# The order of the gated values of two expert rows on VectorE and ScalarE

## The chip, the cores and the metric

The kernel runs as one program on one core of a Trainium2 chip. The metric is the device time of one execution in microseconds (us). Three executions of the kernel before were timed, and one more was profiled.

## The reference

Two transformer blocks are computed for one sequence of 256 tokens of width 1024, in float32. The change lies in the last layer of the second block, a product-key expert layer: 16384 experts, 8 heads, and 16 experts chosen per head and token.

```python
u = jnp.take(expert_down, ei, axis=0)
act = jax.nn.gelu(jnp.einsum("btd,bthkd->bthk", xi, u), approximate=False)
vv = jnp.take(expert_up, ei, axis=0)
return jnp.einsum("bthk,bthkd->btd", (gi * act), vv)
```

After it come the residual sum and one last rmsnorm. `ei` are the experts that were chosen, `gi` their softmax gates.

## The kernel before, in words

The kernel gathers nothing: it computes every expert for every token and multiplies by a gate that is zero where an expert was not chosen. The experts form 128 *rows* of 128 experts. For a row c, `down_gen` computes gelu(down . x) for all 256 tokens, a tile `ge` of 128 experts x 256 tokens (PE into `dps`, then ScalarE). A dense table of gates G lies in device memory and is fetched 8 rows at a time into `gr` (1 MB, three buffers). `hidden(c)` then makes the gated values of two rows, c and c + 1, called a *pair* here, and `ts_row` multiplies a row with the matching 128 x 1024 block of `up`, into four PSUM banks `acc` that run over all 128 rows.

Every float32 operand is split into a high part (rounded, written by ScalarE) and a low part (the rest, written by VectorE), and a product is three matmuls: high.high, low.high, high.low. The names are:

- `ge`: the gelu of a row, then, in place, the gated value (VectorE, SCALAR_TENSOR_TENSOR `ge<-ge,gr`).
- `ph`, `pl`: high and low part of the gated values of a pair (ScalarE ACTIVATE `ph<-ge`; VectorE TENSOR_TENSOR `pl<-ge,ph`). Two buffers each.
- `wr`: a raw weight load of two rows (1 MB, three buffers), issued on SP's queue; `wh`, `wl`: high and low part of one row of weights (ScalarE `wh<-wr`; VectorE `wl<-wr,wh`). Three buffers each, a buffer for a row.
- `held`: the same for the last four rows of `up`, which have buffers of their own.

A row costs PE 12 matmuls of 512 columns (2 token tiles x 2 halves x 3 products), so a pair costs 24.

The stage has three parts. While rows of `down` are left, each pass of the loop in `experts` does one pair of `up` rows and two rows of `down` (26 passes). Then 36 passes do `up` rows alone. The last two pairs (rows 124 to 127) aren't multiplied in the loop: their weights go to `held`, and `final` (line 1932) multiplies them token tile by token tile (12 matmuls of pair 124, 12 of pair 126 for tile 0, then 24 for tile 1), so that the last norm of tile 0 can run beside the matmuls of tile 1.

The order on every engine is the order in which the program issues the work. In a pass, `hidden(c + 2)` comes ahead of the matmuls of pair c (line 1715), and a planner (`top_up`, line 300) issues the splits of the weights some rows ahead of their use, by a model of when their inputs are there. In an `up`-only pass ScalarE thus gets ph, ph, wh, wh, and VectorE ge, pl, ge, pl, wl, wl. An engine runs its instructions in this order, and one that waits holds up all that stand behind it. Nearly all VectorE and ScalarE work is recorded through one helper, line 123; matmuls are line 163, loads line 173.

Of the kernel before, what the change touches and what calls it, by code (L numbers as in the profile page):

```python
# [9 lines left out]
F32 = mybir.dt.float32  # L10
# [4 lines left out]
AF = mybir.ActivationFunctionType  # L15
ALU = mybir.AluOpType
# [110 lines left out]
class Net:  # L127
# [1545 lines left out]
    def experts(self, tab, down, gd):  # L1673
        ve, a = self.ve, self.a
        acc = self.acc4()

        G = gd.tile([N_EXP_CH // GC, P, S, GC], F32, name="G")
        with self.tc.tile_pool(name="pb", bufs=3) as pb:
            self.weave([self.build_G(G, tab, pb, acc)], self.some(down, RING - KEEP))

        groups = []

        def fetch():
            if len(groups) < N_EXP_CH // GC:
                t = gr.tile([P, S, GC], F32, tag="gr", name="gr")
                self.clock.slot("gr", 3, t)
                self.load(t, G[len(groups)])
                groups.append(t)

        def hidden(c):  # L1690

            ph = pw.tile([P, 2, S], F32R, tag="ph", name="ph")
            pl = pw.tile([P, 2, S], F32R, tag="pl", name="pl")
            for e in range(2):
                g = self.ge.pop(c + e)
                ve.scalar_tensor_tensor(out=g, in0=g, scalar=1.0 / GSC, in1=groups[c // GC][:, :, c % GC + e],
                                        op0=ALU.mult, op1=ALU.mult)
                self.split_to(ph[:, e, :], pl[:, e, :], g)
            return ph, pl

        with self.tc.tile_pool(name="pw", bufs=2) as pw, self.tc.tile_pool(name="ph", bufs=1) as pool:
            views = pool.tile([P, 8, 1024], F32R, name="held")
            hold = [[views[:, 2 * j, :], views[:, 2 * j + 1, :]] for j in range(4)]
            self.hold = lambda: hold.pop(0)
            late = []
            with self.tc.tile_pool(name="gr", bufs=3) as gr:
                for n in range(KEEP - 3, -1, -2):
                    self.drain(self.some(down, RING - n))
                    fetch()
                self.drain(self.some(down, RING))  # L1710
                p = hidden(0)
                for c in range(0, N_EXP_CH, 2):
                    cur, last = p, c >= N_EXP_CH - 4
                    if c + 2 < N_EXP_CH:
                        p = hidden(c + 2)
                    if c % GC == GC - 2:
                        fetch()
                    if last:
                        late.append(([self.take("u") for _ in range(2)], cur))
                    else:  # L1720
                        for e in range(2):
                            self.ts_row(acc, self.take("u"), cur[0], cur[1], e, c == 0 and e == 0, False)
                    for _ in range(2):
                        self.drain(self.some(down, len(self.ge) + 1))
            self.hold = None
            self.final(acc, late)
# [393 lines left out]
```

## Time and profile before

| | us |
|---|---|
| three timed executions | 1568.54, 1565.62, 1569.11 (median 1568.54) |
| the profiled execution | 1565.99 |
| its span, first to last instruction | 1564.2 |
| passes with `up` and `down` | 1037.6 to 1329.7 |
| passes with `up` alone | 1329.7 to 1539.9 |
| the last four rows on PE | 1539.9 to 1556.0 |
| last norm of tile 1 and its store | 1556.0 to 1564.2 |

Times in the trace count from the first instruction of the span. Engines are PE (TensorE matmul), PEld (its weight load), DVE (VectorE), ACT (ScalarE), POOL and SP. Matmuls overlap in the pipeline: one of 512 columns is shown with 0.39 us, and the next starts some 0.23 us after it, so PE's pace is read from the starts. Idle time is shown with what ended it; where an instruction waits for two things, the one named is the one that came last by the trace's reckoning.

### The profile page before, as it was taken

The page shows a single profiled execution, that of the slowest core. Times are in us where ns is not written, and L with a number is a line of the kernel's source. Part 1 is how long each engine was busy: PE and PEld are TensorE (multiplying, and loading weights), DVE is VectorE, ACT ScalarE, POOL GpSimd, SP SyncE. Part 2 cuts the span into 40 slices and gives each one's busy share as a digit, 9 for nine tenths or more (in the row PEclk, how much of TensorE's full clock was granted, in tenths as well). Part 3 has the DMA queues.
Part 4 walks back from the last instruction along what each step waited for, and adds up shares of the span by engine and source line. Part 5 has one row for each costly group of instructions (what it writes and reads, how often), then busy time and mean ns, then how long its engine had stood idle before and what let it go on. Part 6 is the DMA issues. An engine that isn't in the chain of part 4 may idle for free.

```text
span 1564.2 us, 25831 instructions
## 1 busy us (share of the span) xinstructions
PE 1501.6 (96%) x10234; PEld 1351.0 (86%) x10234; DVE 1043.1 (67%) x1949; ACT 779.8 (50%) x1295; POOL 450.8 (29%) x354
## 2 busy tenths in 40 slices
PE   8999899999999999999999999899999999999997
PEld 7878888998698989898999999899999999877775
DVE  6567454646668887556798877755656565777776
ACT  5655444555555342346556555544545454444443
POOL 4433643445666555467780000000000000000000
PEclk9999999999999999999999999999999999999999
DMA  6652555555434333256445687876666555665652
GB/s 229 234 182 59 191 186 188 187 190 193 180 113 139 131 109 109 95 176 255 162 160 191 216 250 240 271 263 216 215 216 216 204 200 216 238 220 215 226 178 94
DMA packets 103785, 295.35 MB, mean 189 GB/s; under 512 B 5744, under 2 KB 39024, under 8 KB 100720
## 3 DMA queue, kind: packets, MB, share of 16 engines
q1 hardware_dynamic: 70640, 276.93, 50.4%
q10 hardware_dynamic: 33024, 16.78, 3.7%
q8 instruction: 80, 1.31, 0.3%
q14 instruction: 41, 0.34, 0.1%
HBM read 275.86 MB, written 17.83 MB: 188 GB/s over the span
## 4 chain that ended last, share of the span: by engine, by line
PE 68%; DVE 16%; ACT 6%; issue 6%; POOL 2%; DMA 1%; SPq 0%; ACTq 0%; POOLq 0%; DVEq 0%
PE dps L163 21%; PE acc L163 18%; PE wsps L163 13%; PE fps L163 4%; DVE wl L123 3%; ACT wh L123 3%; PE yps L163 3%; DVE ge L123 3%; POOL wl L123 1%; ACT ph L123 1%; DVE eq L123 1%; DVE pl L123 1%; DVE rt L123 1%; PE tp L168 1%; PE pu L163 1%
## 5 line engine op out<-in xcount | busy, mean ns | idle before, releaser
L123 DVE TENSOR_TENSOR wl<-wr,wh 128x1024 fp32r<-128x1024 f32 (+1 forms) x298 | 365.3, 1245 | 193.2 <-ACT wh L123 192.8
L123 ACT ACTIVATE wh<-wr 128x1024 fp32r<-128x1024 f32 (+1 forms) x436 | 445.0, 1040 | 53.1 <-ACT wh L123 25.6
L123 POOL TENSOR_TENSOR wl<-wr,wh 128x512 fp32r<-128x512 f32 (+2 forms) x276 | 367.1, 1354 | 312.2 <-ACT wh L123 301.3
L163 PE MATMUL dps<-xh,wh 128*128 128x256 f32 x1024 | 251.5, 283 | 0.0
L163 PE MATMUL dps<-xl,wh 128*128 128x256 f32 x1024 | 251.3, 283 | 0.0
L123 POOL TENSOR_TENSOR xn<-h,gain 128x512 f32<-128x512 f32 x4 | 5.1, 1274 | 742.9 <-DVE h L123 737.3
L163 PEld LDWEIGHTS dps<-xl,wh 128*128 128x128 f32 x1024 | 196.7, 192 | 1.0
L163 PEld LDWEIGHTS dps<-xh,wh 128*128 128x128 f32 x1024 | 196.6, 192 | 1.0
L163 PE MATMUL acc<-wh,ph 128*128 128x512 f32 x496 | 196.1, 395 | 0.9 <-ACT ph L123 0.8
L163 PE MATMUL acc<-wh,pl 128*128 128x512 f32 x496 | 194.0, 391 | 0.0
L163 PE MATMUL wsps<-xh,wh 128*128 128x256 f32 x680 | 178.9, 298 | 0.0
L163 PE MATMUL wsps<-xl,wh 128*128 128x256 f32 x680 | 171.9, 288 | 0.0
L163 PE MATMUL acc<-wl,ph 128*128 128x512 f32 x496 | 156.6, 397 | 2.0
L163 PE MATMUL dps<-xh,wl 128*128 128x256 f32 x1024 | 145.3, 284 | 2.3 <-DVE wl L123 1.4
L123 ACT ACTIVATE ge<-dps 128x256 f32<-128x256 f32 x128 | 49.2, 384 | 187.0 <-PE dps L163 186.9
L163 PEld LDWEIGHTS wsps<-xh,wh 128*128 128x128 f32 x680 | 133.7, 197 | 1.2 <-issue 0.4
L163 PEld LDWEIGHTS dps<-xh,wl 128*128 128x128 f32 x1024 | 131.9, 192 | 2.9 <-DVE wl L123 1.6
L163 PEld LDWEIGHTS wsps<-xl,wh 128*128 128x128 f32 x680 | 133.9, 197 | 0.1
L123 ACT ACTIVATE ph<-ge 128x256 fp32r<-128x256 f32 x128 | 53.5, 418 | 145.1 <-DVE ge L123 111.1
L163 PEld LDWEIGHTS acc<-wl,ph 128*128 128x128 f32 x496 | 90.7, 188 | 32.7 <-DVE wl L123 15.3
L163 PEld LDWEIGHTS acc<-wh,ph 128*128 128x128 f32 x496 | 93.2, 188 | 25.9 <-ACT wh L123 7.1
L163 PEld LDWEIGHTS acc<-wh,pl 128*128 128x128 f32 x496 | 93.3, 188 | 18.2 <-DVE pl L123 0.3
(437 smaller groups left out, 2606.6 us busy)
## 6 DMA issues: line engine op xcount, KB each, us to landing
wr<-in_down_dram SPq DMA_DIRECT2D x64, 1024.0 KB, 5.0
wr<-in_up_dram SPq DMA_DIRECT2D x64, 1024.0 KB, 5.0
wr<-in_w_in_a_dram SPq DMA_DIRECT2D x35, 1024.0 KB, 4.9
wr<-in_w_mlp_out_dram SPq DMA_DIRECT2D x16, 1024.0 KB, 4.9
G<-st ACTq DMA_DIRECT2D x16, 1024.0 KB, 6.0
gr<-G SPq DMA_DIRECT2D x16, 1024.0 KB, 6.9
wr<-in_w_mlp_in_dram SPq DMA_DIRECT2D x14, 1024.0 KB, 5.0
wr<-in_w_z_dram SPq DMA_DIRECT2D x8, 1024.0 KB, 4.9
```

The costliest lines, as they stand in the source:

```text
L123: return f(*args, **kw)
L163: self.nc.tensor.matmul(out=out, lhsT=lhsT, rhs=rhs, start=start, stop=stop)
L168: self.nc.tensor.transpose(out, in_, self.ident[:in_.shape[0], :in_.shape[0]])
```

## The change

In `hidden`, the two gated values are made first (each followed, on the other engine, by its high part), and then both low parts. The operations, their operands and their count stay the same. 

```diff
-            for e in range(2):
-                g = self.ge.pop(c + e)
+            gs = [self.ge.pop(c + e) for e in range(2)]
+            for e, g in enumerate(gs):
                 ve.scalar_tensor_tensor(out=g, in0=g, scalar=1.0 / GSC, in1=groups[c // GC][:, :, c % GC + e],
                                         op0=ALU.mult, op1=ALU.mult)
-                self.split_to(ph[:, e, :], pl[:, e, :], g)
+                self.ac.activation(out=ph[:, e, :], in_=g, func=AF.Copy)
+            for e, g in enumerate(gs):
+                ve.tensor_tensor(out=pl[:, e, :], in0=g, in1=ph[:, e, :].bitcast(F32), op=ALU.subtract)
             return ph, pl
```

VectorE in one `up`-only pass, pair 120 (`ge_14336` and `ge_14367` are its two rows, `wl_16100` and `wl_16116` the low parts of its weights). Before:

```order
L123 SCALAR_TENSOR_TENSOR ge_14336<-ge_14336,gr_15759 128x256
L123 TENSOR_TENSOR pl_16090<-ge_14336,ph_16089 128x256
L123 SCALAR_TENSOR_TENSOR ge_14367<-ge_14367,gr_15759 128x256
L123 TENSOR_TENSOR pl_16090<-ge_14367,ph_16089 128x256
L123 TENSOR_TENSOR wl_16100<-wr_16013,wh_16099 128x1024
L123 TENSOR_TENSOR wl_16116<-wr_16013,wh_16115 128x1024
```

VectorE at the same place, now:

```order
L123 SCALAR_TENSOR_TENSOR ge_14336<-ge_14336,gr_15759 128x256
L123 SCALAR_TENSOR_TENSOR ge_14367<-ge_14367,gr_15759 128x256
L123 TENSOR_TENSOR pl_16090<-ge_14336,ph_16089 128x256
L123 TENSOR_TENSOR pl_16090<-ge_14367,ph_16089 128x256
L123 TENSOR_TENSOR wl_16100<-wr_16013,wh_16099 128x1024
L123 TENSOR_TENSOR wl_16116<-wr_16013,wh_16115 128x1024
```

The second gated value moves ahead of the first low part; it is so in all 64 pairs. ScalarE's order there (ph, ph, wh, wh) and PE's, POOL's and SP's in the whole program are as before.

The one other difference lies at the end of the loop, on VectorE and ScalarE alike. VectorE before (`ge_14550`, `ge_14581` are pair 124, `ge_14656`, `ge_14687` pair 126; `wr_16097` holds the weights of pair 124, `wr_16139` those of pair 126):

```order
L123 TENSOR_TENSOR held_11647<-wr_16097,held_11647 128x1024 x2
L123 SCALAR_TENSOR_TENSOR ge_14550<-ge_14550,gr_15759 128x256
L123 TENSOR_TENSOR pl_16178<-ge_14550,ph_16177 128x256
L123 SCALAR_TENSOR_TENSOR ge_14581<-ge_14581,gr_15759 128x256
L123 TENSOR_TENSOR pl_16178<-ge_14581,ph_16177 128x256
L123 TENSOR_TENSOR held_11647<-wr_16139,held_11647 128x1024 x2
L123 SCALAR_TENSOR_TENSOR ge_14656<-ge_14656,gr_15759 128x256
L123 TENSOR_TENSOR pl_16214<-ge_14656,ph_16213 128x256
L123 SCALAR_TENSOR_TENSOR ge_14687<-ge_14687,gr_15759 128x256
L123 TENSOR_TENSOR pl_16214<-ge_14687,ph_16213 128x256
```

VectorE there now:

```order
L123 TENSOR_TENSOR held_11647<-wr_16097,held_11647 128x1024 x2
L123 TENSOR_TENSOR held_11647<-wr_16139,held_11647 128x1024
L123 SCALAR_TENSOR_TENSOR ge_14550<-ge_14550,gr_15759 128x256
L123 SCALAR_TENSOR_TENSOR ge_14581<-ge_14581,gr_15759 128x256
L123 TENSOR_TENSOR pl_16180<-ge_14550,ph_16179 128x256
L123 TENSOR_TENSOR pl_16180<-ge_14581,ph_16179 128x256
L123 TENSOR_TENSOR held_11647<-wr_16139,held_11647 128x1024
L123 SCALAR_TENSOR_TENSOR ge_14656<-ge_14656,gr_15759 128x256
L123 SCALAR_TENSOR_TENSOR ge_14687<-ge_14687,gr_15759 128x256
L123 TENSOR_TENSOR pl_16214<-ge_14656,ph_16213 128x256
L123 TENSOR_TENSOR pl_16214<-ge_14687,ph_16213 128x256
```

The planner's reckoning of time moved too, and it puts the split of row 126 ahead of the gated values of pair 124. ScalarE has the same: before held x2, ph x2 (pair 124), held x2, ph x2 (pair 126); now held x3, ph x2, held, ph x2.

## Rows read from the trace of the kernel before

**Rows 1.** Page, part 1: busy us, share of the span, instructions.

```profile
PE 1501.6 (96%) x10234; PEld 1351.0 (86%) x10234; DVE 1043.1 (67%) x1949; ACT 779.8 (50%) x1295; POOL 450.8 (29%) x354
```

**Rows 2.** Windows: stretch, us, busy us of each engine, PEclk, DMA share, GB/s.

```profile
1100.00:1200.00 100.00, 100.00 (x644) 91.50 (x643) 60.36 (x72) 48.25 (x72) 0.00 (x0) 1.00 0.60 211
1329.67:1343.30 13.63, 13.63 (x63) 11.27 (x62) 10.04 (x15) 6.21 (x10) 0.00 (x0) 1.00 0.69 240
1343.30:1539.92 196.62, 194.50 (x806) 146.19 (x804) 145.05 (x200) 92.13 (x134) 0.00 (x0) 1.00 0.58 208
1539.92:1546.37 6.45, 3.94 (x15) 2.39 (x14) 4.88 (x8) 2.73 (x4) 0.00 (x0) 1.00 0.00 0
1546.37:1549.79 3.42, 3.42 (x9) 2.67 (x8) 0.62 (x2) 0.42 (x1) 0.00 (x0) 0.50 0.58 153
1549.79:1555.95 6.16, 6.15 (x27) 4.70 (x25) 4.36 (x14) 2.35 (x6) 1.47 (x2) 1.00 0.00 0
```

**Rows 3.** Waits of PEld, 1343 to 1540: us in total, times, longest.

```profile
PEld acc L163 <- DVE wl L123: 15.3, 31, 0.5
PEld acc L163 <- ACT wh L123: 7.1, 30, 0.5
```

**Rows 4.** Waits of DVE, 1332 to 1540.

```profile
DVE pl L123 <- ACT ph L123: 36.3, 70, 0.8
DVE wl L123 <- ACT wh L123: 18.4, 35, 0.5
```

**Rows 5.** Timeline of DVE, one pass: start us, us, what; in brackets idle before.

```profile
1406.42 0.66 DVE L123 SCALAR_TENSOR_TENSOR ge<-ge,gr 128x256 f32<-128x256 f32 x1
1407.62 0.43 DVE L123 TENSOR_TENSOR pl<-ge,ph 128x256 fp32r<-128x256 f32 x1 [0.55 <-ACT ph L123]
1407.96 0.64 DVE L123 SCALAR_TENSOR_TENSOR ge<-ge,gr 128x256 f32<-128x256 f32 x1
1409.08 0.42 DVE L123 TENSOR_TENSOR pl<-ge,ph 128x256 fp32r<-128x256 f32 x1 [0.48 <-ACT ph L123]
1410.04 2.36 DVE L123 TENSOR_TENSOR wl<-wr,wh 128x1024 fp32r<-128x1024 f32 x2 [0.53 <-ACT wh L123]
1412.31 0.67 DVE L123 SCALAR_TENSOR_TENSOR ge<-ge,gr 128x256 f32<-128x256 f32 x1
```

**Rows 6.** Timeline of ACT, the same pass.

```profile
1407.17 0.42 ACT L123 ACTIVATE ph<-ge 128x256 fp32r<-128x256 f32 x1 [2.11 <-PE acc L163]
1408.63 0.42 ACT L123 ACTIVATE ph<-ge 128x256 fp32r<-128x256 f32 x1 [1.05 <-DVE ge L123]
1408.96 1.99 ACT L123 ACTIVATE wh<-wr 128x1024 fp32r<-128x1024 f32 x2
```

**Rows 7.** Chain that ended last, 1332 to 1564: first and last of 33.

```profile
1345.95 1.22 DVE wl L123
...
1535.11 1.22 DVE wl L123
```

**Rows 8.** Timeline of PE: a row's first matmul (three rows), first matmul of `final`.

```profile
1329.67 0.40 PE L163 MATMUL acc<-wh,ph 128*128 128x512 f32 x1
...
1332.41 0.39 PE L163 MATMUL acc<-wh,ph 128*128 128x512 f32 x1
...
1343.30 0.39 PE L163 MATMUL acc<-wh,ph 128*128 128x512 f32 x1
...
1539.92 0.39 PE L163 MATMUL acc<-held,ph 128*128 128x512 f32 x1
```

**Rows 9.** Tiles `wh` and `gr`, 1330 to 1540: duration min/median/max in ns.

```profile
L123 DVE TENSOR_TENSOR wl<-wr,wh x70: 1216/1222/1228, 1333.1 to 1535.1; 128x1024 fp32r<-128x1024 f32 x70
L123 DVE SCALAR_TENSOR_TENSOR ge<-ge,gr x71: 630/651/681, 1329.5 to 1538.5; 128x256 f32<-128x256 f32 x71
```

**Rows 10.** Waits of SP's queue, 1330 to 1564, and DMA issues there.

```profile
SPq L173 <- DVE wl L123: 170.8, 34, 5.5
wr<-in_up_dram SPq DMA_DIRECT2D x34, 1024.0 KB, 5.0
```

**Rows 11.** Last four rows: the wait of PE, the split of pair 124 on DVE.

```profile
PE acc L163 <- ACT ph L123: 2.5, 1, 2.5
1536.25 2.35 DVE L123 TENSOR_TENSOR held<-wr,held 128x1024 fp32r<-128x1024 f32 x2
```

## The prediction

> **What bounds the kernel now.** I read the busy shares first: PE is busy 96% of the span [rows 1], so a change on DVE and ACT pays only where PE waits, or is paced, by them. The windows by stage come next. While `up` and `down` rows alternate PE is busy 100.00 of 100 us [rows 2]: there the 26 pairs can gain nothing. In the passes with `up` alone PE still reads 194.50 of 196.62 us busy [rows 2], which looks full, but a matmul's duration covers part of the gap behind it. So I go by starts: the first five rows of this stage, 60 matmuls, start between 1329.67 and 1343.30 [rows 8], which is 0.2272 us a matmul, 2.73 a row, 5.45 a pair. From there on the chain of waits shows the low part of a pair's second weight row 33 times, from 1345.95 to 1535.11 [rows 7]: 189.16 / 32 = 5.91 us a pair. PE waits 31 times for `wl` and 30 for `wh` [rows 3], at every pair. The stage is paced by something 0.46 us slower than PE.
>
> That is the ring between DVE and ACT. In one pass [rows 5, 6]: DVE makes the first gated value (1406.42), ACT its high part (1407.17), DVE waits 0.55 and makes the low part (1407.62), then the second value (1407.96), ACT its high part (1408.63), and only behind that in ACT's order come the high parts of the weights (1408.96), on which DVE's 2.36 us of `wl` wait (1410.04), and behind these the next pair's first value (1412.31). Once round is 5.89 us. DVE is busy for 145 of the 197 us [rows 2], but all its idle time stands in this ring: 36.3 us for `ph` in 70 waits, 18.4 for `wh` in 35 [rows 4].
>
> **The change part by part.** No instruction is added or removed. In the ring the second gated value moves ahead of the first low part.
>
> Step 1, the new ring, with the durations and distances of that pass. First value 1406.42 to 1407.08, its high part 1407.17 to 1407.59, as before. The second value starts 0.09 us before the end of the instruction ahead of it, as it did behind `pl`: 1406.99 to 1407.63. Its high part follows 0.03 later (1408.63 behind 1408.60 before): 1407.66 to 1408.08. The first low part has its input at 1407.62 as before and ends at 1408.05; the second starts 0.03 behind the second high part, 1408.11, and ends at 1408.53. `wh` starts 0.33 after that high part's start, 1407.99; `wl` 1.08 after that, 1409.07, by when DVE is free. It ends at 1411.43, and the next first value starts at 1411.34. Once round is 4.92 us instead of 5.89: what goes is 0.97, the first low part and most of the wait for `ph`.
>
> Step 2, what is late next. 4.92 is under PE's 5.45, so PE sets the pace and 0.53 us a pair remains as slack. The stage's 36 pairs then take 36 x 5.452 = 196.3 us from 1329.67 and end at 1525.95 instead of 1539.92 [rows 8]: 13.97 us.
>
> Can the buffers hold PE's pace? The row three back frees `wh` and `wl`, two row times (5.45 us) before a row starts; `wh` and then `wl` need some 1.05 + 1.2 of that. `ph` comes free when the pair two back ends, one pair time ahead. And the loads: SP waits 34 times for `wl` to free a `wr` buffer, 170.8 us in all [rows 10], so it is ahead; a load lands in 5.0 us, and with three buffers of a pair there is more than a pair time. At PE's pace in the first 13.63 us the DMA moved 240 GB/s at a share of 0.69 [rows 2], so the rate asked for has been there. Cost: nothing.
>
> Step 3, an overlap that the trace before doesn't show: the second value runs on DVE beside the first high part on ACT. The nearest rows are `wl`, of which one runs beside `wh` and one mostly alone: 1216 to 1228 ns over 70 of them [rows 9], no stretch. The gated values themselves lie between 630 and 681 [rows 9]. So from 0 to 0.05 us a pair, and I take 0; even ten times the upper end would just use up the slack of 0.53. A gain is excluded since a pair runs at PE's pace either way.
>
> Step 4, the last four rows. PE's 48 matmuls start at 1539.92 and the last one ends at 1555.95 [rows 2, 8]; at 0.2272 each they take 48 x 0.2272 + 0.16 (a last one lasts 0.39) = 11.07 instead of 16.03: 4.96 us are lost there. 2.5 of them are one wait for `ph` of pair 126 [rows 11]. Behind this idle the granted clock is 0.50, the lower level of 1.2 GHz, for 3.42 us [rows 2], which is 1.71 us of work. The rest, 0.75, are short waits at pair 124. All three come from DVE arriving late out of the ring. Once it has slack, take T as the time when PE ends pair 122. The weight buffer for row 123 comes free at T - 8.2 (three rows), its `wl` ends about T - 5.9. Then DVE has three `held` splits at 1.18 [rows 11], to T - 2.4; two values, to T - 1.1; two low parts, the second of them when ACT has given the high part, to T - 0.2. The last `held` waits for ACT, which has it at T + 0.4 behind the high parts of pair 124, and ends at T + 1.6; the next value ends at T + 2.2 and its high part at T + 2.6. PE asks for that after 12 matmuls, T + 2.73. It asks for the low part at T + 2.95 and gets it about T + 3.1: a wait of 0.15 at most, too short beside the 2.5 to expect the lower clock. The moved `held` split costs 1.2 us of DVE ahead of pair 124's values; the slack covers it, and without cover it would make PE start pair 124 later by about as much. Gain 4.8, bounds 0 and 4.96.
>
> Step 5, the first pair, where PE waits for `hidden(0)`: the first high part is where it was, the first low part 0.02 later at most (step 1). Nothing.
>
> Behind PE's last matmul the norm of tile 1 stays as it is. The sum: 13.97 + 4.8 = 18.8 us off the profiled execution's 1565.99 (span 1564.2 and 1.8 around it), 1547.2. That execution lies 2.6 under the median of the three timed ones, 1568.54, and the four together have their middle at 1567.3; I set the sum against that: 1548.5.
>
> **The rivals.** A is the forecast. B: the middle gains, the end doesn't. If DVE doesn't get ahead in time, PE still idles before pair 126 and the clock still falls: 1567.3 - 14.0 = 1553.3, or between the two. For it: the end's slack is a sum of small distances, and the order there changed as well. Against it: 0.53 us a pair over 36 pairs.
>
> C: nothing comes of it, because buffers and not the order make the ring. ACT's rows say so on their face: the first `ph` shows 2.11 us idle ended by "PE acc" [rows 6], as if PE had still to free a buffer. Then ACT would start no earlier and the time stays at 1567.3. Against it: `ph` starts 0.09 us behind the end of the gated value, 1407.08, whichever releaser is named, and PE is itself waiting for `wh` and `wl` [rows 3]. The Trainium skill, Perfetto Trace Analysis, section Optimization Strategy, says that the same gap repeated on the engine that should be full can mean that there are too few buffers for the next tile. By that rule the order would be worth nothing and the sum would be 1567.3; by the row it is 18.8 us. The gap does repeat here, but its releasers are splits and not PE, so this trace doesn't bear the rule out.
>
> D, slower: DVE and ACT, now reading the same tile side by side, hold each other up. The place is the second value beside the first high part and the second high part beside the first low part. Decisive is 0.97 us a pair, what the ring gains. If the second value (0.64) and its high part (0.42) took twice as long the ring would be 5.98, 0.07 a pair over 36 pairs: 1567.3 + 2.5, with later starts at the end 1571. The rows of `wl` speak against it (step 3).
>
> **How the numbers follow.** A 0.76, B 0.14, C 0.05, D 0.03; 0.02 for a middle gain of half the size. A measurement of this kernel tells about 0.2% (3.1 us) from no change. A, B and the half gain are faster: 0.92. C is the same: 0.05. D is slower: 0.03. The range goes from A against the lowest execution with 2 us for scatter, 1565.6 - 18.8 - 2 = 1544.8, to B with as much, about 1556.
>
> **What would show it.** In the profile after: DVE's wait `pl<-ph` in the `up`-only passes falls from 36.3 us to a few; one pair takes 5.45 us there, and PE's waits for `wl` and `wh` go; ACT's and DVE's idle is now ended by PE, since they wait for buffers; the last rows start near 1526; PE has no idle of 2.5 us there and the clock stays at 1.00. Step 1 is wrong if a pair still takes 5.9 with the same instructions in the new order; step 2 if a pair takes between 5.5 and 5.9 and PE waits for a load or a buffer; step 4 if PE still idles before pair 126 while the middle has sped up. A time above 1560 would make the reading of the ring wrong.

## The result and the profile after

Four executions of each kernel are compared: before 1568.54, 1565.62, 1569.11 and 1561.81 us (median 1567.08), after 1547.85, 1544.70, 1548.35 and 1546.56 us (median 1547.20). The ratio is 0.9872, with a 95% interval of 0.9857 to 0.9887: some 20 us faster, between 17.7 and 22.4. The forecast was 1548.5.

The profiled execution after has a span of 1546.1 us, 18.1 less than the one before. Its busy shares hardly tell the two apart; this line answers to [rows 1]:

```profile
PE 1487.0 (96%) x10234; PEld 1355.1 (88%) x10234; DVE 1043.8 (68%) x1949; ACT 784.8 (51%) x1295; POOL 450.4 (29%) x354
```

The windows by stage do, with the same columns as [rows 2]: the passes with `up` and `down`, all the passes with `up` alone, the last four rows, and what follows them.

```profile
1100.00:1200.00 100.00, 100.00 (x645) 91.52 (x645) 59.71 (x73) 49.98 (x72) 0.00 (x0) 1.00 0.59 209
1330.90:1526.76 195.86, 195.86 (x866) 162.17 (x865) 158.01 (x218) 102.78 (x147) 0.00 (x0) 1.00 0.63 226
1526.76:1537.81 11.05, 11.04 (x49) 8.80 (x47) 7.52 (x19) 3.12 (x8) 1.41 (x2) 1.00 0.18 47
1537.81:1546.07 8.26, 0.00 (x0) 0.00 (x0) 3.16 (x12) 1.94 (x5) 1.15 (x1) 0.70 0.34 128
```

The `up`-only passes take 195.86 us instead of 210.25 (1329.67 to 1539.92 before): 14.4 less. The last four rows take 11.05 instead of 16.0: 5.0 less, at a granted clock of 1.00 throughout. The first stage doesn't change, and neither does the end behind PE's last matmul (8.26 and 8.3). Against these 19.4 us stands that the `up` passes begin 1.23 us later in this execution, as the whole expert stage does; that lies ahead of the changed code, and the start of this stage lies between 1033.5 and 1038.9 in the profiled executions below.

VectorE over one pass, against [rows 5]:

```profile
1406.40 1.20 DVE L123 SCALAR_TENSOR_TENSOR ge<-ge,gr 128x256 f32<-128x256 f32 x2
1407.74 0.78 DVE L123 TENSOR_TENSOR pl<-ge,ph 128x256 fp32r<-128x256 f32 x2
1409.04 1.23 DVE L123 TENSOR_TENSOR wl<-wr,wh 128x1024 fp32r<-128x1024 f32 x1 [0.52 <-ACT wh L123]
1410.70 1.23 DVE L123 TENSOR_TENSOR wl<-wr,wh 128x1024 fp32r<-128x1024 f32 x1 [0.44 <-ACT wh L123]
1411.85 1.23 DVE L123 SCALAR_TENSOR_TENSOR ge<-ge,gr 128x256 f32<-128x256 f32 x2
```

ScalarE in the same pass, against [rows 6]:

```profile
1407.28 0.77 ACT L123 ACTIVATE ph<-ge 128x256 fp32r<-128x256 f32 x2 [2.05 <-PE acc L163]
1407.96 1.04 ACT L123 ACTIVATE wh<-wr 128x1024 fp32r<-128x1024 f32 x1
1409.61 1.06 ACT L123 ACTIVATE wh<-wr 128x1024 fp32r<-128x1024 f32 x1 [0.61 <-PE acc L163]
```

The two values, the two high parts and the two low parts each run through without a gap. From one pass to the next it is 5.45 us (1406.40 to 1411.85), not 5.89. The waits between 1332 and 1526 answer to [rows 4]; first VectorE's, then ScalarE's:

```profile
DVE wl L123 <- ACT wh L123: 32.9, 69, 0.5
DVE pl L123 <- ACT ph L123: 0.2, 1, 0.2
```

```profile
ACT ph L123 <- PE acc L163: 69.9, 34, 2.2
ACT wh L123 <- PE acc L163: 20.1, 34, 0.6
ACT ph L123 <- DVE ge L123: 2.7, 2, 2.5
```

The wait `pl<-ph` is gone (36.3 to 0.2; with the gaps for which the view names no releaser, VectorE is idle for 4.5 us ahead of `pl`). ScalarE is now held by PE twice a pass: `ph` and the second `wh` wait for a buffer that PE still reads. Before, "PE acc" stood beside `ph` too, but there `ph` came 0.09 us behind the gated value; now it comes 0.23 us behind it (1406.40 and 0.65 for the first value, to 1407.28), and PE is the one waited for. For [rows 3] and the PE line of [rows 11] there is nothing to show: PE and its weight loads wait for nobody from 1325 us to the end. The chain of waits says the same in one line:

```profile
1331.99 205.83 PE acc L163 x908
```

### The profile page after: what moved, and what is told of

It reads as the page before. It is cut to its first block, busy times and chain, and to the rows that moved or that the text cites. A ratio compares the mean times of both kernels' runs of the same rounds, so it can differ in the third digit from the quotient of the medians.

```text
span 1546.1 us, 25831 instructions
## 1 busy us (share of the span) xinstructions
PE 1487.0 (96%) x10234; PEld 1355.1 (88%) x10234; DVE 1043.8 (68%) x1949; ACT 784.8 (51%) x1295; POOL 450.4 (29%) x354
## 3 DMA queue, kind: packets, MB, share of 16 engines
q8 instruction: 80, 1.31, 0.3%
## 4 chain that ended last, share of the span: by engine, by line
PE 80%; DVE 11%; ACT 3%; issue 3%; POOL 2%; DMA 1%; SPq 0%; DVEq 0%; POOLq 0%; ACTq 0%
PE acc L163 30%; PE dps L163 21%; PE wsps L163 13%; PE fps L163 4%; PE yps L163 3%; POOL wl L123 1%; ACT wh L123 1%; DVE eq L123 1%; DVE rt L123 1%; PE tp L168 1%; PE pu L163 1%; POOL hl L123 1%; PE ops L163 1%; PE sc L163 1%; DVE wl L123 1%
## 5 line engine op out<-in xcount | busy, mean ns | idle before, releaser
L123 ACT ACTIVATE wh<-wr 128x1024 fp32r<-128x1024 f32 (+1 forms) x436 | 451.8, 1043 | 92.6 <-PE acc L163 69.6
L163 PE MATMUL acc<-wl,ph 128*128 128x512 f32 x496 | 152.8, 389 | 0.0
L163 PEld LDWEIGHTS acc<-wh,ph 128*128 128x128 f32 x496 | 93.2, 188 | 19.4 <-ACT ph L123 1.0
L163 PE MATMUL wsps<-xh,wl 128*128 128x256 f32 x680 | 98.4, 288 | 0.0
```

Of the source, the lines that this page charges most:

```text
L123: return f(*args, **kw)
L163: self.nc.tensor.matmul(out=out, lhsT=lhsT, rhs=rhs, start=start, stop=stop)
```

## The experiments

The theory: in the `up`-only passes VectorE and ScalarE pass work to each other in a ring of 5.9 us a pair. The new order makes it 4.92, below PE's 5.45, and the slack carries over into the last four rows. The rivals: the new order helps everywhere a little; buffers that PE holds make the ring; the last rows gain by the order that the planner changed there; GpSimd or VectorE contention eats what is gained. Each kernel was timed beside the kernel before and profiled once; the ratios are to the kernel before, with 95% intervals. Where a diff below has a condition, the new order of the change stands under it and the old one under the else. "Up-only passes" is the time from their first matmul to the first one of the last four rows, "last four rows" from there to the end of PE.

**New order from row 52 on (shown), and new order up to there (c < 52).**

```diff
+            if c >= 52:
...
+            else:
...
```

> New order only for pairs from row 52 on, that is in the passes with up alone and the last four rows; the 26 passes before keep the old order. Theory (the DVE-ACT ring paces the up-only passes and nothing else): the whole gain, ratio to the kernel before 0.987, up-only passes 196 us, last four rows on PE 11 us. Rival (the earlier low start of the second value helps everywhere a little): about half the gain, 0.993.

> New order only for the pairs of rows 0 to 51, made in the passes with up and down rows. Theory: no change, ratio 1.000 within 0.2%, up-only passes 210 us, last four rows 16 us. Rival (helps everywhere): 0.993.

From row 52 on: ratio 0.9883 (0.9856 to 0.9911), `up`-only passes 195.87 us, last four rows 11.06: the whole gain. Up to row 52: 0.9995 (0.9981 to 1.0010), 210.24 and 15.96 us. The second shows where the wait goes. VectorE's waits from 1040 to 1325, in the passes with `up` and `down`, first with the old order there (the first of these kernels), then with the new one:

```profile
DVE wl L123 <- ACT wh L123: 86.9, 76, 2.3
DVE pl L123 <- ACT ph L123: 24.2, 50, 0.5
```

```profile
DVE wl L123 <- ACT wh L123: 110.4, 77, 2.4
DVE pl L123 <- ACT ph L123: 1.7, 7, 0.5
```

The same wait goes here as well, 22.5 us of it, and the next wait on the same engine takes 23.5 more. These passes last 292.06 us either way, since PE is full. The rival that it helps everywhere falls.

**Three buffers for the high part, old order.**

```diff
-            ph = pw.tile([P, 2, S], F32R, tag="ph", name="ph")
+            ph = pw.tile([P, 2, S], F32R, tag="ph", name="ph", bufs=3)
```

> Old order, three buffers for the high part of the gated values instead of two. Theory (the order makes the ring; the buffer was free, and 'ended by PE acc' is only the name of the second semaphore): no change, ratio 1.000 within 0.2%, a pair still 5.9 us. Rival C (ACT waits for PE to free the buffer): most of the gain, 0.988 to 0.991, a pair 5.45 us.

Ratio 0.9977 (0.9965 to 0.9988), `up`-only passes 207.85 us, 5.835 a pair, last four rows 15.60. The buffer rival falls: the passes gain 2.4 of 14.4 us. But "no change" was wrong too. Its ScalarE in one pass:

```profile
1412.09 0.42 ACT L123 ACTIVATE ph<-ge 128x256 fp32r<-128x256 f32 x1 [2.06 <-DVE ge L123]
1413.55 0.42 ACT L123 ACTIVATE ph<-ge 128x256 fp32r<-128x256 f32 x1 [1.04 <-DVE ge L123]
1413.88 2.00 ACT L123 ACTIVATE wh<-wr 128x1024 fp32r<-128x1024 f32 x2
```

and its VectorE:

```profile
1411.39 0.67 DVE L123 SCALAR_TENSOR_TENSOR ge<-ge,gr 128x256 f32<-128x256 f32 x1
1412.54 0.43 DVE L123 TENSOR_TENSOR pl<-ge,ph 128x256 fp32r<-128x256 f32 x1 [0.48 <-ACT ph L123]
```

The first `ph` starts 0.03 us behind the end of the value (1411.39 + 0.67 = 1412.06 to 1412.09), where it was 0.09 [rows 5, 6]. With a third buffer the program has no wait for PE at this instruction any more. The wait cost 0.06 us in 34 of the 36 pairs though PE had long been done, and 0.34 in one, for a reason that stays open; together that is the 2.4 us.

**One more operation in the ring (shown), and two (2 in place of the first 1).** The result of the added operation is read by nobody.

```diff
                 self.ac.activation(out=ph[:, e, :], in_=g, func=AF.Copy)
+                for _ in range(1 if e == 0 else 0):
+                    junk = pw.tile([P, S], F32, tag="pj", name="pj")
+                    ve.scalar_tensor_tensor(out=junk, in0=self.x[0][:, 0, :].bitcast(F32), scalar=1.0, in1=groups[c // GC][:, :, c % GC + 1],
+                                            op0=ALU.mult, op1=ALU.mult)
```

> The new order with one more VectorE multiply of 128x256 between the two gated values of each pair, into a scratch tile that nobody reads. Theory (ring 4.92 us, PE 5.45, slack 0.53): the ring gets about 0.57 longer, 5.49, just over PE: 0 to 3 us slower than the changed kernel, ratio to the kernel before 0.987 to 0.989. Rival (the ring is far below PE's pace, or the slack comes from buffers): no DVE wait for ACT's split of the gated values appears and nothing changes at all; rival (no slack): 0.57 x 36 = 20 us, ratio 1.000.

> The same with two more multiplies. Theory: the ring is 4.92 + 1.14 = 6.06 us, above PE's 5.45 and above the old 5.91; up-only passes 213 to 216 us, the last four rows again 16 us, total 2 to 6 us above the kernel before, ratio 1.003. Rival (DVE has much room, it was busy for 74% of these passes only): nothing or 1 us above the changed kernel, 0.988.

The time of a pair is read here on VectorE, from pass to pass. One more: ratio 0.9885 (0.9869 to 0.9902), a pair 5.483 us (forecast 5.49), `up`-only passes 196.40. Two more: 1.0041 (1.0022 to 1.0059), a pair 6.082 (forecast 6.06), passes 216.28 (forecast 213 to 216), last four rows 15.51, and PE waits again, 32 times each for `wl` and `wh`. VectorE with one more:

```profile
1410.21 0.65 DVE L123 SCALAR_TENSOR_TENSOR ge<-ge,gr 128x256 f32<-128x256 f32 x1
1410.77 0.67 DVE L123 SCALAR_TENSOR_TENSOR pj<-xh,gr 128x256 f32<-128x256 f32 x1
1411.34 0.66 DVE L123 SCALAR_TENSOR_TENSOR ge<-ge,gr 128x256 f32<-128x256 f32 x1
```

The added operation moves the second value by 0.57 us (1410.77 to 1411.34). With none the passes run at PE's 5.44 and the ring can't be seen; with one it is 5.48, with two 6.08. Back from these by 0.57 and 1.14 it is 4.91 and 4.94 us, what step 1 had worked out (4.92). So the slack is 0.5 us a pair, and DVE, busy for 158 of 196 us, has no more room than that. With one more operation the last four rows take 13.45 us instead of 11.05, and PE waits there for `ph` and `pl` for 1.8 us in four waits, at a granted clock of 1.00. That part was not in the expectation. Two things stand behind it. VectorE ends the last low part of the passes 4.5 us before PE begins the last rows, where it was 6.0 in the changed kernel and 3.6 in the kernel before: 36 pairs at 0.04 us over PE's pace have used up 1.5 us of its lead. And the added operations stand in the last two pairs too, one of them (0.57 us) ahead of the first high part of pair 126.

**The last two pairs in the old order (shown), and only they in the new (c >= 124).**

```diff
+            if c < 124:
...
+            else:
...
```

> New order everywhere but in the last two pairs, rows 124 to 127. Theory (the end gains because DVE comes out of the up-only passes with slack): up-only passes 196 us; at the end each old pair costs DVE some 0.97 us again, so the high part of pair 126 comes about 0.5 us after PE asks for it; no lower clock; last four rows 11.5 to 12 us, total 0.5 to 1 us above the changed kernel. Rival (the end gains by its own order): the 2.5 us wait and the lower clock are back, last four rows 16 us, total 5 us above it.

> New order only in the last two pairs. Theory: up-only passes stay 210 us; at the end DVE is late by about 2 x 0.97 us less, so PE waits for pair 126 some 0.6 to 1.5 us instead of 2.5; last four rows 12 to 14 us, total 2 to 4 us under the kernel before, ratio 0.998. Rival (the end gains by its own order): last four rows 11 us, ratio 0.9968.

Old order at the end: ratio 0.9896 (0.9875 to 0.9917), passes 195.87, last four rows 12.04 us, and PE's wait there is

```profile
PE acc L163 <- ACT ph L123: 0.4, 1, 0.4
```

close to the forecast of 0.5 us. New order only at the end: 0.9996 (0.9982 to 1.0011), passes 210.21, last four rows 15.02. PE still waits

```profile
PE acc L163 <- ACT ph L123: 1.7, 1, 1.7
```

and the granted clock still falls, as the windows over these rows show:

```profile
1538.28:1544.10 5.82, 4.14 (x17) 2.72 (x17) 4.92 (x8) 3.02 (x5) 0.00 (x0) 1.00 0.07 5
1544.10:1547.51 3.41, 3.41 (x10) 2.64 (x9) 0.00 (x0) 0.00 (x0) 0.00 (x0) 0.50 0.42 145
1547.51:1553.30 5.79, 5.79 (x26) 4.46 (x24) 4.36 (x14) 2.29 (x6) 1.41 (x2) 1.00 0.00 0
```

The expectation of 12 to 14 us counted 0.97 us twice. From the start of the `held` splits of pair 124 to the first high part of pair 126 it is 1536.25 to 1545.14 = 8.89 us before and 1534.62 to 1542.55 = 7.93 here: 0.96, once. Only pair 124's values stand ahead of that high part; pair 126's own order leaves it where it is. Both kernels say that the end gains by the slack that comes out of the passes ahead, 4.0 of 5.0 us with the values at the end row by row as before, and 1.0 by their new order alone. ScalarE shows that high part in the kernel before, with the new order only at the end, and with the old order only there:

```profile
1545.14 0.42 ACT L123 ACTIVATE ph<-ge 128x256 fp32r<-128x256 f32 x1 [2.09 <-DVE ge L123]
```

```profile
1542.55 0.87 ACT L123 ACTIVATE ph<-ge 128x256 fp32r<-128x256 f32 x2 [2.09 <-DVE ge L123]
```

```profile
1529.18 0.42 ACT L123 ACTIVATE ph<-ge 128x256 fp32r<-128x256 f32 x1 [1.93 <-DVE ge L123]
```

Behind PE's first matmul of the last rows (1539.92, 1538.30 and 1526.39) it starts after 5.2, 4.3 and 2.8 us; in the changed kernel it is 1.9. This also answers the rival of the planner's order. The `held` split that it moved is in its new place in the third of these kernels and in its old place in the second, so no run has it apart from the slack. But the high part comes 2.4 us earlier in the third kernel than in the kernel before, and so does the last low part of the passes, which ends 6.0 instead of 3.6 us ahead of that matmul. The moved split adds nothing to that.

**The low part on GpSimd, row by row.**

```diff
-                self.split_to(ph[:, e, :], pl[:, e, :], g)
+                self.ac.activation(out=ph[:, e, :], in_=g, func=AF.Copy)
+                self.po.tensor_tensor(out=pl[:, e, :], in0=g, in1=ph[:, e, :].bitcast(F32), op=ALU.subtract)
```

> Row by row as before, but the low part of the gated values on GpSimd instead of VectorE, so that VectorE no longer waits for it. Theory (the wait in DVE's order was the cost, not the place of the instruction): the ring is as short as with the new order, up-only passes 196 us, ratio 0.987. Rival (GpSimd and VectorE hold each other up): VectorE's instructions get longer than 1.22 and 0.65 us, or PE waits for the low part; between 0.988 and 1.003.

Ratio 0.9874 (0.9857 to 0.9890), `up`-only passes 195.87 us. So what cost was the low part in VectorE's order, and it can be taken out of the ring in another way. The wait and the 0.34 us of the instruction itself go together here, as they do with the new order; no run parts them. VectorE and GpSimd in one pass:

```profile
1407.77 1.20 DVE L123 SCALAR_TENSOR_TENSOR ge<-ge,gr 128x256 f32<-128x256 f32 x2
1410.41 1.31 DVE L123 TENSOR_TENSOR wl<-wr,wh 128x1024 fp32r<-128x1024 f32 x1 [1.43 <-ACT wh L123]
1412.07 1.23 DVE L123 TENSOR_TENSOR wl<-wr,wh 128x1024 fp32r<-128x1024 f32 x1 [0.35 <-ACT wh L123]
```

```profile
1409.19 1.44 POOL L123 TENSOR_TENSOR pl<-ge,ph 128x256 fp32r<-128x256 f32 x2 [4.00 <-ACT ph L123]
```

The `wl` that starts while GpSimd is still at the second low part (the two share 0.2 us) takes 1.31 us, the other 1.23: a little contention, if that is the cause, and the slack takes it. The last four rows take 11.39 us instead of 11.05, since the first matmul with a low part of pair 126 starts 0.2 us late. At the first pair, where nothing covers a wait, PE waits 1.3 us for GpSimd's low part, and the passes with `up` and `down` take 293.39 us instead of 292.06. It is no better than the change.

## Why the prediction was right

Step 1, the ring: right. 4.92 us was read off one pass by moving its pieces, and the two kernels with added operations give 4.91 and 4.94. Moving the second value ahead takes the first low part and the wait for its high part out of the ring; where only those passes have the new order the whole gain is there, and where only the others have it, none.

Step 2, PE's pace is next: right. 36 pairs in 195.86 us are 5.441 a pair, against 5.452 from the five rows at the start of the stage; 14.4 us gained for a forecast of 13.97, the rest being that pace. Buffers and loads hold it: PE waits for nothing. Of the sign that ScalarE's and VectorE's idle time is now ended by PE, ScalarE's half holds; VectorE's is still ended by `wh` (32.9 us), behind a ScalarE that PE holds.

Step 3, two engines side by side: right. The values take 631 to 673 ns (median 648) in these passes after, 630 to 681 before; high and low parts have medians of 418 and 426 ns as before. Rival D falls with it.

Step 4, the end: right, 5.0 us for a forecast of 4.8. The distances held as well, as the timeline after shows for the low part of row 123's weights, PE's first matmul of the last rows (T) and the two high parts of pair 126:

```profile
1519.50 1.23 DVE L123 TENSOR_TENSOR wl<-wr,wh 128x1024 fp32r<-128x1024 f32 x1 [0.44 <-ACT wh L123]
...
1526.76 0.39 PE L163 MATMUL acc<-held,ph 128*128 128x512 f32 x1
...
1528.62 0.91 ACT L123 ACTIVATE ph<-ge 128x256 fp32r<-128x256 f32 x2 [1.94 <-DVE ge L123]
```

The weights' low part ends at T - 6.0 (forecast T - 5.9); the first high part ends at T + 2.3 (forecast T + 2.6, with PE's demand at T + 2.73), and PE doesn't wait. The clock drop went with the wait of 2.5 us. Which waits bring it isn't settled: after one of 1.7 us in the kernel with the new order at the end only the clock fell to 0.50, after one of 1.7 us in the kernel with two more operations it stayed at 1.00, as it did with waits up to 0.6 us. Rival B had the condition right (without the slack of the passes, with the new order at the end only, the last rows still take 15.0 us) but the slack was there.

Rival C, buffers: it fell as a mechanism, but not to zero. Three buffers give 0.23%, through the wait that they spare and not through the buffer. The 0.09 us that the prediction read as `ph` right behind its value held 0.06 of that wait. The rule of the Trainium skill (Perfetto Trace Analysis, Optimization Strategy) that a repeated gap can mean too few buffers pointed the wrong way in this case: the third buffer gave 2.4 us in the passes, the order 14.4. No other buffer was tried; with the new order the same buffers carry PE's pace. The row with `ph` right behind its value was the better witness.

The total: 19.4 us by stages for a forecast of 18.8, the difference being PE's pace (0.4) and the end (0.2); the medians moved by 19.9, with an interval of 17.7 to 22.4.

## What to carry to other kernels

When two in-order engines feed each other, write the round trip down from one pass of the timeline and see which pieces lie on it: an engine that is busy for three quarters of the time can still set the pace, and then the order of its instructions counts, not their sum. Move a consumer behind the next producer and the wait goes without any work being saved; do it where the ring is longer than the pace of the engine that should bind, since elsewhere the wait only moves to the next instruction. To measure slack that no profile shows, add one operation and then two to the ring.

## What the runs showed of the hardware

In these kernels a wait for PE beside the one for VectorE delays the ACTIVATE `ph` by 0.06 us even where PE has long been done: it starts 0.09 us behind its value with that wait and 0.03 without it, in 34 of the 36 pairs of the `up`-only passes (one more starts 0.37 behind, unexplained, and 0.03 without the wait). All of it is 2.4 us (0.2%) while the ring binds. The releaser that the profile names there ("PE acc") is then not the one that held the instruction.

A further wait doesn't cost that everywhere: a pair's first `wl` waits for ScalarE and for PE too and starts 0.03 us behind its `wh`. In the trace of the kernel before, the two differ in which wait stands in a semaphore instruction of its own ahead of the work. For `ph` it is the late one, for VectorE (at 1407.11 in the pass of [rows 6], the ACTIVATE 0.06 us behind it); for `wl` it is the early one, for PE, which is over by then. That this order is what costs is not tested.
